# RWKV stage of a hybrid backbone on one core: TensorE in the emitted order, both halves of an inverse stage in one PSUM tile, and the parts of a unit at other places of its period

## The chip, the core and the metric

The kernel runs on one core of a Trainium2 chip. A core has a matrix engine (TensorE, called PE in the rows), VectorE (DVE), ScalarE (ACT), GpSimd (POOL) and SyncE (SP), which here issues DMAs; each works through its own list of instructions and waits at semaphores for the others. The metric is the device time of one execution in microseconds (us); the lower the better.

## The reference, cut to what matters

One trunk layer over 512 latent tokens with 256 context tokens ahead of them, model width 2048: a modulated norm, one input projection for three groups of recurrent heads (GLA, mLSTM, RWKV-7), one output projection, then a mixture of experts. The change lies in the RWKV heads, 12 of width 64 with one scan per direction:

```python
def _rwkv_scan(inp, s0):
    """RWKV-7: S = S diag(w) + (S (-kk)) (kk*a)^T + v k^T ; y = S r."""
    r, decay, k, v, kk, a = (jnp.moveaxis(t, 1, 0) for t in inp)
    def step(s, t):
        rt, wt, kt, vt, kkt, at = t
        sa = jnp.einsum('bhvk,bhk->bhv', s, -kkt)
        s = (s * wt[:, :, None, :] + sa[..., None] * (kkt * at)[:, :, None, :]
             + vt[..., None] * kt[:, :, None, :])
        return s, jnp.einsum('bhvk,bhk->bhv', s, rt)
    s_fin, ys = lax.scan(step, s0, (r, decay, k, v, kk, a))
    return jnp.moveaxis(ys, 0, 1), s_fin
```

Each output is then normalised per head, scaled, given a bonus term and gated:

```python
yr_l = (_head_norm(yl, g_norm, RWKV_GN_EPS, True) + bl) * jax.nn.sigmoid(gl)
```

## The kernel before

The scan is done in chunks of 64 tokens. A unit is one of three groups of four heads (two rows of 128 partitions, both directions) times one of six blocks of 128 tokens, so there are 18 units. A unit has three parts, each a Python generator that yields between pieces of its work.

`rw_s1` loads keys, values and decays (SyncE), forms decays by a product with a triangle (`pb`, the rows `g<-tri,rv_sgh`) and three exponentials on ScalarE (`ex`), multiplies them into `BK` and `AR` (VectorE and GpSimd), makes the key-query products `pA` in two rounds (rows `g<-AR,BK`), masks them on VectorE into `AMa` and `AMr` (L734), writes the 16x16 diagonal blocks of `AMa` to memory (`s_ad`, eight DMAs, L741) and reads them back in another layout (`Lay`, L742), and transposes `BK` (`pT`, L750).

`rw_s2` inverts a 64x64 triangle per chunk and head. First the 16x16 diagonal blocks: 15 steps of a product and a reduction on VectorE, `ptm<-Tm,Lay` (L776) and `Tm<-ptm` (L778), here called the T steps. The result goes through memory (`s_td`) by 16 DMAs into `ed`, two block-diagonal arrays `E` and `Dd`. Then four **inverse stages** on TensorE (L806), each a product over eight chunks: `Y` (from `Bo` and `Dd`, copied out of PSUM by ScalarE as `iY`, L810), `F1`, `F2` and `Ef` (each evacuated by VectorE with an addition, L812; the rows name the first two `iF`). A stage is emitted as two halves of four chunks, each half in a PSUM tile of its own under the tag "g", which has three buffers, with two yields in a half.

`rw_s3` carries the state through the unit's two chunks: `pX` (L833) gives `chX`, then `pSA` (L843) gives the two writes to `rv` (ScalarE L845, VectorE L846), then `pS` (L853) gives the new state `chS`. Every sixth unit ends with `rwkv_fin` for two rows of heads, four pieces in all with 256 columns each: a centering (L943), a square `fin_sq` on ScalarE, the sums `nb` (L152), a rsqrt chain on VectorE and GpSimd to `nb_x` (L159), its transposes (L167) and products.

`rwkv_all` runs periods: in period k it weaves `rw_s1` of unit k, `rw_s2` of unit k-1 and `rw_s3` of unit k-2 with `fill`, which is the rest of the input projection: matmuls `pl<-hil,wh` and the like (L329), six in a step, whose weights are split by ScalarE (`wh`, L306) and GpSimd or VectorE (`wl`, L307). `weave` gives each generator a number of steps and a share of the period and always advances the one that lags. What it emits is then ordered by a scheduler, which may move instructions against the emitted order by their priority; part of the projection's matmuls are emitted at high priority. The eight PSUM banks of this stage are: "g" three, "ch" two, "acc" one, "pl" two.

Of the kernel before, what the change touches and what calls it, by code (L numbers as in the profile page):

```python
# [19 lines left out]
P = 128  # L20
# [3 lines left out]
LC = 256  # L24
# [11 lines left out]
NS2 = 45  # L36
# [6 lines left out]
NKE = (12, 12, 12, 12)  # L43
# [5 lines left out]
W1, W2, W3 = (0, .9), (0, 1), (0, 1)  # L49


class Kern:
    def __init__(self, tc, I, out):
        self.tc, self.nc, self.I, self.out = tc, tc.nc, I, out
        self.dram = {}
        self.gt1 = None

# [20 lines left out]
    def load_consts(self, cp, ps):  # L78
# [42 lines left out]
        with self.tc.tile_pool(name="prow", bufs=1) as pr:  # L121
            done = 0
            rest = list(order)
            while done < tot:
# [12 lines left out]
                nc.tensor.transpose(p[:, :used], vr[:used], self.ident[:used, :used])  # L137
# [7 lines left out]
    def norm_bcast(self, pool, ps, tag, sq, nt, scale, eps, op, bufs=2):  # L145
# [5 lines left out]
        for t in range(nt):  # L151
            nc.tensor.matmul(pn[:, t], sq[:, t * P:(t + 1) * P], self.ind2, start=True, stop=True)  # L152
# [10 lines left out]
        for t0 in range(0, nt, 4):  # L163
            n = min(4, nt - t0)
            p = ps.tile([P, 512], F32, name=tag, bufs=bufs)
            for t in range(n):
                nc.tensor.transpose(p[:, t * P:(t + 1) * P], rx[:, t0 + t], self.ident)  # L167
# [3 lines left out]
    def phase_h(self, ps, early):  # L171
# [13 lines left out]
        with tc.tile_pool(name="wa", bufs=5) as wa, tc.tile_pool(name="xp", bufs=1) as xp:  # L185
            for t in range(6):
# [10 lines left out]
                for k0 in range(0, KT, 4):  # L197
                    p = ps.tile([P, 4, P], F32, name=("pl", "pc")[k0 // 4 % 2], bufs=self.pb)
                    for k in range(4):
                        nc.tensor.transpose(p[:, k], xt[:, (k0 + k) * P:(k0 + k + 1) * P], self.ident)  # L200
# [4 lines left out]
            for j in range(4):  # L205
                pa = ps.tile([P, 256], F32, name="px", bufs=2)
                for k0 in range(0, KT, 2):
# [3 lines left out]
                    for k in range(2):  # L211
                        for s in range(2):
                            for hf in range(2):
                                b = 32 * (2 * s + hf)
                                nc.tensor.matmul(pa[b:b + 32, :], self.sil[:, k0 + k, :], w[:, s, k, hf * 256:(hf + 1) * 256],
# [7 lines left out]
                for q in range(2):  # L223
                    nc.tensor.transpose(pt[:, q], ar[:, q * P:(q + 1) * P], self.ident)
# [36 lines left out]
    def ada2_sum(self, blk):  # L261
        nc = self.nc
        for q in range(4):
            p = self.ps.tile([P, 512], F32, name="px", bufs=2)
            nc.tensor.matmul(p[:1], self.ones[:, :1], self.acc2[:, q], start=True, stop=True)
# [44 lines left out]
    def w_tile(self, col, n, lat, ctx, fill=None):  # L310
# [4 lines left out]
        for q in range(4):  # L315
# [113 lines left out]
    def rw_k(self, pr):  # L429
# [25 lines left out]
        for d in range(2):  # L455
            yield
            a = sp.tile([P, T], F32, name="o_a")
            for (s0, n) in ((0, LC), (LC, S)):
                p = ps.tile([P, 512], F32, name="px", bufs=2)
                nc.tensor.matmul(p[:, :n], wz[:96, 1, d], self.wa1[:96, 2 + d, s0:s0 + n], start=True, stop=True)  # L460
# [11 lines left out]
            for t0 in (0, 4):  # L472
                n = min(4, 6 - t0)
                p = ps.tile([P, 4, P], F32, name="px", bufs=2)
                for t in range(n):
                    nc.tensor.matmul(p[:, t], self.wa1[:97, d, (t0 + t) * P:(t0 + t + 1) * P], wz[:, 0, d], start=True, stop=True)
# [20 lines left out]
    def to_tokens(self, x, o):  # L497
# [3 lines left out]
        for t0 in range(0, nt, 4):  # L501
            n = min(4, nt - t0)
            p = self.ps.tile([P, 4, P], F32, name=tag, bufs=bufs)
            for t in range(n):
                nc.tensor.transpose(p[:, t], x[:, (t0 + t) * P:(t0 + t + 1) * P], self.ident)
            nc.vector.tensor_copy(o[:, t0:t0 + n], p[:, :n])

    def rw_r(self, pr):
# [9 lines left out]
        nc.tensor.matmul(p, self.blk, m, start=True, stop=True)  # L518
# [145 lines left out]
    def rw_s1(self, st, u, q, g):  # L664
# [33 lines left out]
        for i in range(2):  # L698
            pb = ps.tile([P, 2, 2, 2, 64], F32, name="g", bufs=3)
            for d in range(2):  # L700
                for j, x in enumerate((sgh, sgl)):
                    nc.tensor.matmul(pb[:, d], x[:, i, d], self.tri, start=(j == 0), stop=(j == 1))
# [14 lines left out]
            yield  # L717
        n = 2 if g > 1 else 1
# [4 lines left out]
        for d in range(2):  # L723
            pA = [ps.tile([P, 4, n, 64], F32, name="g", bufs=3) for _ in range(2)]
            for c in range(4):
                for h in range(2):
                    hs = slice(64 * h, 64 * h + 64)
                    for a in range(2):
                        nc.tensor.matmul(pA[h][64 * a:64 * a + 64, c].rearrange("p a t -> p (a t)"), BK[hs, 4 * d + c, a],
                                         AR[hs, 4 * d + c, :n].rearrange("p a t -> p (a t)"), start=True, stop=True)  # L730
# [15 lines left out]
        pT = [ps.tile([P, 8, 64], F32, name="g", bufs=3) for _ in range(2)]  # L746
        for c in range(8):
            for h in range(2):
                hs = slice(64 * h, 64 * h + 64)
                nc.tensor.transpose(pT[h][:, c], BK[hs, c].rearrange("p a t -> p (a t)"), self.ident[hs, hs])  # L750
# [6 lines left out]
    def rw_s2(self, st, u):  # L757
# [8 lines left out]
        p = ps.tile([P, 8, 64], F32, name="g", bufs=3)  # L766
        for c in range(8):
            for h in range(2):
                hs, ks = slice(64 * h, 64 * h + 64), slice(64 - 64 * h, 128 - 64 * h)
                nc.tensor.matmul(p[hs, c], AMa[ks, h, c], RV[ks, h, c], start=True, stop=True)  # L770
# [13 lines left out]
        for j in range(2):  # L784
# [1328 lines left out]
```

## Time and profile before

| | |
|---|---|
| median of three runs | 3050.22 us (3045.81 to 3050.96) |
| the profiled execution | 3046.72 us, span 3045.0 us |
| mean granted clock of TensorE | 0.957 of full speed |
| TensorE busy | 2764.3 us, 91% of the span |
| VectorE busy | 1597.2 us, 52% |
| the RWKV stage | about 786 to 1560 us of the span |

The span is the profiled time between the first and the last instruction; the execution's own time is 1.7 us longer. [...]

### The profile page before, as it was taken

How to read it: one execution, taken by the hardware profiler on the slowest of the kernel's cores; microseconds unless marked ns; L12 is line 12 of the kernel's file. 1: busy time of each engine (PE TensorE's matmuls, PEld its weight loads, DVE VectorE, ACT ScalarE, POOL GpSimd, SP SyncE). 2: the span in 40 equal slices, each digit the busy share in tenths (PEclk: the TensorE clock that was granted, in tenths of full speed). 3: DMA queues.
4: the chain of work that ended last, by engine and by line, in shares of the span. 5: the costliest groups of instructions: out<-in, count | busy, mean ns of one | idle time of the engine just before them, and what ended most of it. 6: DMA issues, size and time to landing. Idle time of an engine off the chain costs nothing. (4 is left out here: it accounts for less than half of the span.)

```text
span 3045.0 us, 50599 instructions
## 1 busy us (share of the span) xinstructions
PE 2764.3 (91%) x19241; PEld 1811.1 (59%) x19241; DVE 1597.2 (52%) x3215; ACT 811.3 (27%) x1570; POOL 796.0 (26%) x765
## 2 busy tenths in 40 slices
PE   5999998989898998989968888879999999999997
PEld 3477777778676766767746666644444444444442
DVE  4376666686576555545547655643343433434335
ACT  4132332346432233222222322331021111211112
POOL 2332222221443343343344333431010110101101
PEclk8999999998999999999979999989999999999999
DMA  8857788887643343343266321459999999999997
GB/s 305 283 179 226 233 239 248 241 257 220 173 110 97 85 128 95 97 117 98 70 207 197 105 94 49 133 213 409 398 396 408 389 409 395 397 410 395 409 397 290
DMA packets 527741, 730.79 MB, mean 240 GB/s; under 512 B 121137, under 2 KB 343903, under 8 KB 526339
## 3 DMA queue, kind: packets, MB, share of 16 engines
q1 hardware_dynamic: 363696, 640.77, 58.8%
q10 hardware_dynamic: 161927, 81.17, 10.4%
q0 software_dynamic: 1872, 5.57, 0.6%
q8 instruction: 154, 2.52, 0.3%
q14 instruction: 92, 0.75, 0.1%
HBM read 672.50 MB, written 54.93 MB: 239 GB/s over the span
## 5 line engine op out<-in xcount | busy, mean ns | idle before, releaser
L1672 PE MATMUL pgu<-ring,xg 128*64 128x512 f32 x2048 | 480.6, 600 | 0.0
L307 POOL TENSOR_TENSOR wl<-wr,wh 128x512 fp32r<-128x512 f32 x191 | 263.2, 1379 | 668.8 <-ACT wh L306 600.7
L329 PE MATMUL pl<-hil,wh 128*128 128x512 f32 x928 | 404.4, 437 | 4.7 <-ACT hil L241 3.7
L329 PE MATMUL pl<-lol,wh 128*128 128x512 f32 x928 | 376.3, 405 | 0.2
L329 PE MATMUL pl<-hil,wl 128*128 128x512 f32 x928 | 372.4, 401 | 1.1 <-POOL wl L307 1.1
L306 ACT CAST wh<-wr 128x512 fp32r<-128x512 f32 x292 | 179.6, 619 | 528.0 <-PE pl L329 282.0
L1693 POOL TENSOR_TENSOR hl<-h,hh 128x512 fp32r<-128x512 f32 x64 | 83.9, 1311 | 809.7 <-ACT hh L1692 779.4
L1672 PEld LDWEIGHTS pgu<-ring,xg 128*64 128x64 f32 x2048 | 134.4, 136 | 237.3 <-issue 227.4
L1672 PE MATMUL py<-ring,hT 128*64 128x512 f32 x1024 | 230.4, 593 | 2.4 <-DMA ring<-in_moe_w_down_dram 2.4
L259 DVE SCALAR_TENSOR_TENSOR acc<-w,sil,acc 128x512 f32<-128x512 f32 x240 | 201.7, 870 | 58.5 <-DMA w<-in_w_ada_dram 57.6
L329 PEld LDWEIGHTS pl<-hil,wh 128*128 128x128 f32 x928 | 178.8, 193 | 60.7 <-issue 14.6
L329 PEld LDWEIGHTS pl<-hil,wl 128*128 128x128 f32 x928 | 178.8, 193 | 42.4 <-POOL wl L307 2.1
L329 PEld LDWEIGHTS pl<-lol,wh 128*128 128x128 f32 x928 | 179.6, 194 | 38.3 <-issue 6.4
L1672 PEld LDWEIGHTS py<-ring,hT 128*64 128x64 f32 x1024 | 76.7, 137 | 149.4 <-issue 141.9
L329 PE MATMUL pc<-hic,wl 128*128 128x256 f32 x496 | 146.9, 297 | 13.4 <-DVE wl L307 9.4
L329 PE MATMUL pc<-hic,wh 128*128 128x256 f32 x496 | 147.1, 298 | 4.7 <-ACT wh L306 2.6
L329 PE MATMUL pc<-loc,wh 128*128 128x256 f32 x496 | 146.1, 296 | 1.1 <-DVE loc L242 1.1
L1692 ACT CAST hh<-h 128x512 fp32r<-128x512 f32 x128 | 84.7, 663 | 193.7 <-POOL hl L1693 14.8
L776 DVE TENSOR_TENSOR ptm<-Tm,Lay 64x1 f32<-64x1 f32 (+2 forms) x270 | 105.5, 391 | 20.3 <-DMA Lay<-s_ad 10.1
L1410 POOL TENSOR_TENSOR wol<-wo,woh 128x512 fp32r<-128x512 f32 x56 | 74.9, 1341 | 155.8 <-PE acc L1413 91.3
L1763 DVE SCALAR_TENSOR_TENSOR yt<-py,Wsl,g 128x512 f32<-128x512 f32 x64 | 48.0, 750 | 127.4 <-PE py L1672 127.4
L1693 DVE TENSOR_TENSOR hl<-h,hh 128x512 fp32r<-128x512 f32 x64 | 53.2, 830 | 112.0 <-ACT hh L1692 109.5
(2216 smaller groups left out, 5011.6 us busy)
## 6 DMA issues: line engine op xcount, KB each, us to landing
ring<-in_moe_w_gate_dram SPq DMA_DIRECT2D x256, 512.0 KB
ring<-in_moe_w_up_dram SPq DMA_DIRECT2D x256, 512.0 KB
ring<-in_moe_w_down_dram SPq DMA_DIRECT2D x128, 1024.0 KB
wr<-in_w_in_dram ACTq DMA_DIRECT2D x288, 256.0 KB
w<-in_w_ada_dram SPq DMA_DIRECT2D x256, 256.0 KB
w<-in_w_ada_dram SPq DMA_DIRECT2D x64, 512.0 KB
wo<-in_w_out_dram SPq DMA_DIRECT2D x56, 256.0 KB
rv_xk<-d_xk SPq DMA_DIRECT2D x36, 256.0 KB
```

The costliest lines, as they stand in the source:

```text
L259: nc.vector.scalar_tensor_tensor(acc, w, self.sil[:, k, 0:1], acc, op0=OP.mult, op1=OP.add)
L306: nc.scalar.copy(wh[:, :, :n], wr[:, :, :n])
L307: (nc.vector if q in self.wdve else nc.gpsimd).tensor_tensor(wl[:, :, :n], wr[:, :, :n], wh[:, :, :n].bitcast(F32), op=OP.subtract)
L329: nc.tensor.matmul(o[:n], a[:, k, :n], r, start=(q == k == i == 0), stop=(q == k == 3 and i == 2))
L776: nc.vector.tensor_tensor(pt_[:, :t, :t], Tm[:, :t, :t], Lay[:, :t, t].rearrange("q (o s) -> q o s", o=1).to_broadcast([64, t, t]), op=OP. ...
L1410: nc.gpsimd.tensor_tensor(wl, w, wh.bitcast(F32), op=OP.subtract)
L1672: pin(nc.tensor.matmul(*a, **k))
L1692: nc.scalar.copy(hh, h)
L1693: (nc.gpsimd if k else nc.vector).tensor_tensor(hl, h, hh.bitcast(F32), op=OP.subtract)
L1763: nc.vector.scalar_tensor_tensor(yt, py, W, self.g2[:, col[0]:sum(col)], op0=OP.mult, op1=OP.mult)
```

## The change

First, every matmul and transpose goes through a helper (`mm`, `tr`), which during the RWKV stage pins it behind the TensorE instruction that was emitted before it; the high priority of the projection's matmuls goes. Second, `rw_s1` takes the first three quarters of a period and has more yields, between its rounds, and "g" has two buffers. Third, in `rw_s2` the product `XV` and the four inverse stages share one PSUM tile `g2` with one buffer: a stage's two halves lie in that one bank, are emitted one behind the other, and four yields follow. `Dd` is loaded ahead of `E`. Fourth, `rwkv_fin` leaves `rw_s3` and is a generator of its own in the next period, with its PSUM tiles under "ch". PSUM pools and step counts follow. The diff, cut; each remaining hunk only puts `self.mm` or `self.tr` in the place of the call:

```diff
-W1, W2, W3 = (0, .9), (0, 1), (0, 1)
+W1, W2, W3 = (0, .75), (0, 1), (0, 1)
-NS2 = 45
+NS2 = 50
-NKE = (12, 12, 12, 12)
+NKE = (12, 12, 10, 10, 8)
+NF = 40
+    def mm(self, *a, **k):
+        i = self.nc.tensor.matmul(*a, **k)
+        if self.pin:
+            self.tc.keep_in_program_order(i)
...
-                            first = k % self.wk == 0 and i == 0 or self.wk == 1
-                            with nullcontext() if first else self.tc.high_priority():
-                                nc.tensor.matmul(o[:n], a[:, k, :n], r, start=(q == k == i == 0), stop=(q == k == 3 and i == 2))
+                            self.mm(o[:n], a[:, k, :n], r, start=(q == k == i == 0), stop=(q == k == 3 and i == 2))
...
-            pb = ps.tile([P, 2, 2, 2, 64], F32, name="g", bufs=3)
+            pb = ps.tile([P, 2, 2, 2, 64], F32, name="g", bufs=2)
...
             nc.gpsimd.tensor_copy(W[:, cs], ex[:, 2, :, 63])
             yield
+            yield
...
                     nc.vector.tensor_tensor(o[:, h, 4 * d:4 * d + 4], pA[h][:, :, a], self.msk[:, a:a + 1].to_broadcast([P, 4, 64]), op=OP.mult)
+            yield
+            yield
...
-        p = ps.tile([P, 8, 64], F32, name="g", bufs=3)
+        p = ps.tile([P, 8, 64], F32, name="g2", bufs=1)
...
-        for j in range(2):
+        for j in (1, 0):
             src = self.s_td[u, j].rearrange("(c h i) (s t) -> i h s c t", h=2, i=4, s=16)
...
         for (o, lhs, rhs) in ((Y, Bo, Dd), (F1, Y, E), (F2, Y, F1), (Ef, Y, F2)):
+            p = ps.tile([P, 8, 64], F32, name="g2", bufs=1)
             for c0 in (0, 4):
                 sl = slice(c0, c0 + 4)
-                p = ps.tile([P, 4, 64], F32, name="g", bufs=3)
-                for c in range(4):
+                for c in range(c0, c0 + 4):
                     for h in range(2):
                         hs = slice(64 * h, 64 * h + 64)
-                        nc.tensor.matmul(p[hs, c], lhs[hs, c0 + c], rhs[hs, c0 + c], start=True, stop=True)
-                    if c % 2:
-                        yield
+                        self.mm(p[hs, c], lhs[hs, c], rhs[hs, c], start=True, stop=True)
                 if o is Y:
-                    nc.scalar.copy(Y[:, sl], p)
+                    nc.scalar.copy(Y[:, sl], p[:, sl])
                 else:
-                    nc.vector.tensor_tensor(o[:, sl], p, E[:, sl], op=OP.add)
+                    nc.vector.tensor_tensor(o[:, sl], p[:, sl], E[:, sl], op=OP.add)
+            for _ in range(4):
+                yield
...
-            if g == 5:
-                for i in range(2):
-                    yield from self.rwkv_fin(2 * q + i, self.rwy[:, i])
...
-        for k in range(n + 2):
+        def fins(q):
+            for i in range(2):
+                yield from self.rwkv_fin(2 * q + i, self.rwy[:, i])
+        for k in range(n + 3):
...
-            if k >= 2:
-                gs.append((self.rw_s3(st[k - 2], *units[k - 2]), 7 if units[k - 2][1] < 5 else 47, *W3))
+            if 2 <= k < n + 2:
+                gs.append((self.rw_s3(st[k - 2], *units[k - 2]), 7, *W3))
+            if k >= 3 and units[k - 3][1] == 5:
+                gs.append((fins(units[k - 3][0]), NF))
...
-                gs.append((self.rw_s1(st[k], k, *units[k]), 18, *W1))
+                gs.append((self.rw_s1(st[k], k, *units[k]), 24, *W1))
...
-            nb = yield from self.norm_bcast(mp, ps, "g", sq, 2, 1.0 / 64, 64e-5, OP.add, bufs=3)
+            nb = yield from self.norm_bcast(mp, ps, self.ft[0], sq, 2, 1.0 / 64, 64e-5, OP.add, bufs=self.ft[1])
...
+            self.pin = True
             drain([(self.rwkv_all(fill, NA * 16 // WK - RF), 1)])
+            self.pin = False
```

TensorE, stage F1 of an early unit, before. The names before the arrow are the tile written, behind it the tiles read; in brackets stand the semaphores that the row waits for, by the engine that raises them (DMAHW is a DMA), and L329 rows are the projection:

```order
L806 MATMUL g<-ed_6993,iY 64x64 [waits DMAHW5_49,Activation_49]
L806 MATMUL g<-ed_6993,iY 64x64 [waits DMAHW0_49]
L806 MATMUL g<-ed_6993,iY 64x64 x6
L806 MATMUL g<-ed_6993,iY 64x64 [waits Activation_49]
L806 MATMUL g<-ed_6993,iY 64x64 x7
L329 MATMUL pl<-hil,wh 128x512
L329 MATMUL pl<-lol,wh 128x512
L329 MATMUL pl<-hil,wl 128x512
L329 MATMUL pl<-hil,wh 128x512
L329 MATMUL pl<-lol,wh 128x512
L329 MATMUL pl<-hil,wl 128x512
L806 MATMUL g<-iF_7535,iY 64x64 [waits DVE_49]
```

The same stage in the changed kernel, where all matmuls have the helper's line, L61:

```order
L61 MATMUL g_8020<-ed_6993,iY 64x64 [waits DMAHW4_49,DMAHW6_49,DMAHW0_49,Activation_49]
L61 MATMUL g_8020<-ed_6993,iY 64x64 [waits DMAHW5_49,DMAHW7_49,DMAHW3_49,DMAHW1_49]
L61 MATMUL g_8020<-ed_6993,iY 64x64 x6
L61 MATMUL g_8020<-ed_6993,iY 64x64 [waits DVE_49]
L61 MATMUL g_8020<-ed_6993,iY 64x64 x7
L61 MATMUL pl<-hil,wh 128x512
L61 MATMUL pl<-lol,wh 128x512
L61 MATMUL pl<-hil,wl 128x512 [waits Pool_49]
L61 MATMUL pl<-hil,wh 128x512
L61 MATMUL pl<-lol,wh 128x512
L61 MATMUL pl<-hil,wl 128x512
L61 MATMUL g_8054<-iF_7985,iY 64x64 [waits DVE_49]
```

Before, the second half waits for ScalarE, which wrote the second half of its operand `iY`. Now it waits for VectorE, whose addition of the first half (`iF`) reads the tile `g_8020` that both halves write; six matmuls of the projection follow in both.

VectorE, the additions of F1 and F2 of a unit, before; `iF_8004` is F1, `iF_8005` is F2, `ptm` and `Tm` are the T steps of the next unit:

```order
L812 TENSOR_TENSOR iF_8004<-g,ed_6993 128x256 [waits DMAHW3_49,DMAHW4_49,DMAHW2_49,DMAHW5_49,DMAHW1_49,DMAHW6_49,DMAHW0_49,PE_49]
L812 TENSOR_TENSOR iF_8004<-g,ed_6993 128x256 [waits PE_49]
L550 SCALAR_TENSOR_TENSOR o_a<-pl,par,o_a 128x8x63 [waits DVE_49] x2
L812 TENSOR_TENSOR iF_8005<-g,ed_6993 128x256 [waits PE_49]
L776 TENSOR_TENSOR ptm<-Tm,Lay 64x1 [waits DMAHW7_49,Pool_49]
L812 TENSOR_TENSOR iF_8005<-g,ed_6993 128x256 [waits PE_49]
L778 TENSOR_REDUCE Tm<-ptm 64x1 [waits DVE_49]
```

A unit in the changed kernel, where `iF_8464` is F1:

```order
L823 TENSOR_TENSOR iF_8464<-g_8499,ed_6993 128x256 [waits DMAHW4_49,DMAHW5_49,DMAHW2_49,DMAHW6_49,DMAHW1_49,DMAHW7_49,DMAHW0_49,PE_49]
L290 TENSOR_TENSOR ar_t<-ar_t,ar_b 16x512 [waits DMAHW7_49,DMAHW0_49]
L789 TENSOR_TENSOR ptm<-Tm,Lay 64x1 [waits DMAHW1_49]
L291 SCALAR_TENSOR_TENSOR ar_t<-ar_t,ar_g 16x128 [waits DVE_49]
L823 TENSOR_TENSOR iF_8464<-g_8499,ed_6993 128x256 [waits PE_49]
L791 TENSOR_REDUCE Tm<-ptm 64x1 [waits DVE_49]
L873 TENSOR_TENSOR chW<-ch,chS 128x256 [waits PE_49]
L789 TENSOR_TENSOR ptm<-Tm,Lay 64x2x2 [waits DVE_49]
L791 TENSOR_REDUCE Tm<-ptm 64x2 [waits DVE_49]
L789 TENSOR_TENSOR ptm<-Tm,Lay 64x3x3 [waits DVE_49]
```

Before, the first T step, the one that waits for the DMA into `Lay`, stood between the two additions of F2. Now it stands between the two of F1, and further T steps come ahead of F2's additions.

TensorE, two of the last pieces of `rwkv_fin`, before:

```order
L152 MATMUL g<-k_ind_72,fin_sq 128x2 x2
L167 MATMUL g<-ident,nb_x 128x128 x2
L943 MATMUL g<-rv_y,k_blk 128x256
L152 MATMUL g<-k_ind_72,fin_sq 128x2 x2
L167 MATMUL g<-ident,nb_x 128x128 x2
```

And in the changed kernel:

```order
L61 MATMUL ch<-k_ind_72,fin_sq 128x2 x2
L61 MATMUL pl<-hil,wh 128x512
L61 MATMUL pl<-lol,wh 128x512
L61 MATMUL pl<-hil,wl 128x512
L61 MATMUL pl<-hil,wh 128x512
L61 MATMUL pl<-lol,wh 128x512
L61 MATMUL pl<-hil,wl 128x512
L66 MATMUL ch<-ident,nb_x 128x128 x2
```

Before, the transposes of `nb_x` came directly behind the sums `nb` from which they are worked out. Now six matmuls of the projection lie between them.

## Rows read from the trace of the kernel before

**Rows 1.** The page: the span, and busy time of each engine.

```profile
span 3045.0 us, 50599 instructions
...
PE 2764.3 (91%) x19241; PEld 1811.1 (59%) x19241; DVE 1597.2 (52%) x3215; ACT 811.3 (27%) x1570; POOL 796.0 (26%) x765
```

**Rows 2.** Windows: each stretch with its length, then busy us (instructions) by engine.

```profile
786.00:1560.00 774.00, 693.27 (x8434) 527.69 (x8432) 427.16 (x1124) 221.38 (x460) 304.27 (x340) 0.96 0.41 105
...
1980.00:3045.00 1065.00, 1018.06 (x4960) 464.31 (x4958) 425.24 (x743) 185.09 (x329) 108.71 (x92) 0.98 0.96 380
```

**Rows 3.** Groups of TensorE instructions in 786 to 1560 us, costliest first.

```profile
L329 PE MATMUL pl<-hil,wh 128*128 128x512 f32 x478 | 214.7, 449 | 0.0
...
L806 PE MATMUL g<-iF,iY 64*64 64x64 f32 x1152 | 45.4, 226 | 2.6 <-DVE iF L812 2.5
```

**Rows 4.** Waits of TensorE, 786 to 1560: total us, times, longest.

```profile
PE g L167 <- DVE nb_x L159: 14.7, 9, 2.9
PE ch L853 <- DVE rv L846: 14.0, 10, 3.7
PE g L729 <- POOL AR L713: 6.9, 5, 1.9
PE g L729 <- DVE AMr L734: 4.1, 3, 1.9
...
PE g L750 <- DVE AMr L734: 2.9, 1, 2.9
PE ch L853 <- ACT rv L845: 2.9, 2, 1.6
...
PE g L806 <- ACT iY L810: 0.2, 1, 0.2
```

**Rows 5.** Timeline of one unit's inverse stages and projections: start, length (us), engine.

```profile
1113.87 0.68 PE L806 MATMUL g<-ed,Bo 64*64 64x64 f32 x16
...
1114.60 0.37 ACT L810 COPY iY<-g 128x256 f32<-128x256 f32 x1 [0.24 <-PE g L806]
...
1115.78 0.40 PE L329 MATMUL pl<-lol,wh 128*128 128x512 f32 x1
...
1116.01 0.40 PE L329 MATMUL pl<-hil,wl 128*128 128x512 f32 x1
...
1116.34 1.15 PE L806 MATMUL g<-ed,iY 64*64 64x64 f32 x32
...
1117.07 0.92 DVE L812 TENSOR_TENSOR iF<-g,ed 128x256 f32<-128x256 f32 x2 [7.30 <-PE g L806]
```

**Rows 6.** Groups of the other engines in 786 to 1560 us.

```profile
L776 DVE TENSOR_TENSOR ptm<-Tm,Lay 64x1 f32<-64x1 f32 (+2 forms) x270 | 105.5, 391 | 20.3 <-DMA Lay<-s_ad 10.1 <-DMA rv<-d_vt 3.7
...
L778 DVE TENSOR_REDUCE Tm<-ptm 64x1 f32<-64x1 f32 (+2 forms) x270 | 62.0, 230 | 6.7
```

**Rows 7.** Timeline from the last key-query product to the first step of T.

```profile
1107.53 0.45 PE L729 MATMUL g<-AR,BK 64*64 64x128 f32 x8
...
1108.05 1.28 ACT L576 ACT_TABLE_LOAD   x1
...
1109.35 0.41 DVE L734 TENSOR_TENSOR AMr<-g,msk 128x256 f32<-128x256 f32 x1
...
1109.83 4.34 SPq L741 DMA_DIRECT2D s_ad<-AMa  x8
...
1116.06 0.48 SPq L742 DMA_DIRECT2D Lay<-s_ad  x1
...
1119.57 0.15 DVE L776 TENSOR_TENSOR ptm<-Tm,Lay 64x1 f32<-64x1 f32 x1 [1.59 <-DMA Lay<-s_ad]
```

**Rows 8.** Groups of ScalarE in 786 to 1560 us: the exponentials.

```profile
L707 ACT ACTIVATE ex<-g 128x256 f32<-128x256 f32 x36 | 13.8, 384 | 65.7 <-PE g L702 37.7 <-POOL W L716 13.6 <-DVE AR L715 8.0
```

**Rows 9.** Windows of 20 us with columns as in rows 2: two clock dips.

```profile
900.00:920.00 20.00, 19.62 (x169) 15.74 (x170) 14.67 (x32) 5.15 (x10) 8.66 (x9) 0.83 0.46 113
...
1180.00:1200.00 20.00, 16.90 (x187) 12.64 (x187) 4.14 (x12) 6.48 (x14) 5.66 (x5) 0.83 0.48 124
```

More of the change, by code (lines that the diff above doesn't have):

```diff
@@ L1 @@
 import math
-from contextlib import ExitStack, nullcontext
+from contextlib import ExitStack
 from functools import partial
@@ L151, in norm_bcast @@
         for t in range(nt):
-            nc.tensor.matmul(pn[:, t], sq[:, t * P:(t + 1) * P], self.ind2, start=True, stop=True)
+            self.mm(pn[:, t], sq[:, t * P:(t + 1) * P], self.ind2, start=True, stop=True)
         v = pool.tile([P, nt, 2], F32, name="nb_v")
@@ L264, in ada2_sum @@
             p = self.ps.tile([P, 512], F32, name="px", bufs=2)
-            nc.tensor.matmul(p[:1], self.ones[:, :1], self.acc2[:, q], start=True, stop=True)
+            self.mm(p[:1], self.ones[:, :1], self.acc2[:, q], start=True, stop=True)
             nc.scalar.copy(self.acc2[:1, q], p[:1])
@@ L517, in rw_r @@
         p = ps.tile([P, S], F32, name="px", bufs=2)
-        nc.tensor.matmul(p, self.blk, m, start=True, stop=True)
+        self.mm(p, self.blk, m, start=True, stop=True)
         nc.vector.tensor_tensor(m, self.vt[:, 0, LC:], p, op=OP.mult)
@@ L723, in rw_s1 @@
         for d in range(2):
-            pA = [ps.tile([P, 4, n, 64], F32, name="g", bufs=3) for _ in range(2)]
+            pA = [ps.tile([P, 4, n, 64], F32, name="g", bufs=2) for _ in range(2)]
             for c in range(4):
@@ L745, in rw_s1 @@
             nc.gpsimd.tensor_tensor(Bo[hs], AMa[hs, h], self.ndg[hs, None, :].to_broadcast([64, 8, 64]), op=OP.mult)
-        pT = [ps.tile([P, 8, 64], F32, name="g", bufs=3) for _ in range(2)]
+        pT = [ps.tile([P, 8, 64], F32, name="g", bufs=2) for _ in range(2)]
         for c in range(8):
@@ L769, in rw_s2 @@
                 hs, ks = slice(64 * h, 64 * h + 64), slice(64 - 64 * h, 128 - 64 * h)
-                nc.tensor.matmul(p[hs, c], AMa[ks, h, c], RV[ks, h, c], start=True, stop=True)
+                self.mm(p[hs, c], AMa[ks, h, c], RV[ks, h, c], start=True, stop=True)
             if c % 2:
@@ L832, in rw_s3 @@
                     for hs in H:
-                        nc.tensor.matmul(pX[hs, e], AR[hs, 2 * e + c, 0], St[hs, e], start=True, stop=True)
+                        self.mm(pX[hs, e], AR[hs, 2 * e + c, 0], St[hs, e], start=True, stop=True)
                 if g > 1:
@@ L842, in rw_s3 @@
                 for hs in H:
-                    nc.tensor.matmul(pSA[hs, e], Ef[hs, 2 * e + c], X[hs, e], start=True, stop=True)
+                    self.mm(pSA[hs, e], Ef[hs, 2 * e + c], X[hs, e], start=True, stop=True)
             rv = RV.rearrange("p h (e c) k -> p h e c k", c=2)
@@ L864, in rw_s3 @@
                     for h in range(2):
-                        nc.tensor.matmul(pYo[H[h], 2 * e + c], RV[:, h, 2 * e + c], AMr[:, h, 2 * e + c], start=False, stop=(c == 1 and e == 3))
+                        self.mm(pYo[H[h], 2 * e + c], RV[:, h, 2 * e + c], AMr[:, h, 2 * e + c], start=False, stop=(c == 1 and e == 3))
             yield
@@ L941, in center @@
         nc = self.nc
-        p = self.ps.tile([P, y.shape[1]], F32, name="g", bufs=3)
-        nc.tensor.matmul(p, m, y, start=True, stop=True)
+        p = self.ps.tile([P, y.shape[1]], F32, name=self.ft[0], bufs=self.ft[1])
+        self.mm(p, m, y, start=True, stop=True)
         nc.vector.scalar_tensor_tensor(y, p, -scale, y, op0=OP.mult, op1=OP.add)
@@ L1034, in ml_gates @@
         for j in range(6):
-            nc.tensor.matmul(p[:, j], selp[:, j], dm[:, 1], start=True, stop=True)
+            self.mm(p[:, j], selp[:, j], dm[:, 1], start=True, stop=True)
         nc.vector.tensor_copy(self.mdec, p)
@@ L1252, in gla_pair @@
                     for i in range(2):
-                        nc.tensor.matmul(p, la[:, i, t], lev[:, c0:c0 + 384], start=(i == 0), stop=(i == 1))
+                        self.mm(p, la[:, i, t], lev[:, c0:c0 + 384], start=(i == 0), stop=(i == 1))
                     if j == 0:
@@ L1412, in out_cols @@
                     for t in range(4):
-                        nc.tensor.matmul(po[t], a[:, i, t * P:(t + 1) * P], b, start=(i == j == 0), stop=(i == n - 1 and j == 2))
+                        self.mm(po[t], a[:, i, t * P:(t + 1) * P], b, start=(i == j == 0), stop=(i == n - 1 and j == 2))
                 yield
@@ L1455, in out_last @@
                     for j, (a, b) in enumerate(((yh, wh), (yl, wh), (yh, wl))):
-                        nc.tensor.matmul(p, a[:, i, t * P:(t + 1) * P], b[:, i, cs], start=(i == j == 0), stop=(i == n - 1 and j == 2))
+                        self.mm(p, a[:, i, t * P:(t + 1) * P], b[:, i, cs], start=(i == j == 0), stop=(i == n - 1 and j == 2))
                 nc.vector.tensor_tensor(self.x1[:, t, cs], self.x1[:, t, cs], p, op=OP.add)
@@ L1480, in route_setup @@
         p = self.ps.tile([P, 36], F32, name="lt", bufs=1)
-        nc.tensor.matmul(p, self.ones, sr, start=True, stop=True)
+        self.mm(p, self.ones, sr, start=True, stop=True)
         nc.vector.tensor_tensor(self.cb, self.cb, p, op=OP.add)
@@ L1577, in route_slots @@
         for t in range(4):
-            nc.tensor.matmul(pc, ltb[:, 1], Ab[:, t], start=(t == 0), stop=(t == 3))
+            self.mm(pc, ltb[:, 1], Ab[:, t], start=(t == 0), stop=(t == 3))
         self.over = rp.tile([P, 32, 7], F32, name="over")
```

74 lines of the change are left out of this document (41 added, 33 removed).

## The prediction

> **What bounds the kernel now.** I began with the page: TensorE is busy for 91% of the span [rows 1], so time is lost or won where it idles, switches or runs at half clock. The windows then split the span. In the RWKV stage, 774 us long, TensorE is busy for 693.27 us with a granted clock of 0.96, so about 81 us are idle and about 31 us (4% of 774) are lost to the lower clock level [rows 2]. The last stage is busy for 1018 of 1065 us and the change doesn't touch it [rows 2]. TensorE's order ahead of the RWKV stage is the same in both programs and behind it nearly so; I put every term into the 774 us.
>
> Inside the stage the projection is the bulk: one of its three groups is 214.7 us [rows 3]. It depends on nothing in a unit, so it can fill any gap that the order leaves for it. That makes the list of waits the view to read next. Its 23 rows, from 14.7 us down to 0.2, sum to 69 us: 14.7 for `nb_x` in the final norm, 16.9 for `rv` in the state chain (14.0 and 2.9), 6.9 for `AR`, 7.0 for `AMr` under the products and the transposes (4.1 and 2.9), the rest in small rows [rows 4]. The inverse stages, which the change rebuilds, hardly wait: 2.6 us idle ahead of 1152 matmuls of the later stages [rows 3]. The reader should see that the change can win at most some 69 us of waits, part of 31 us of clock, and the switches below.
>
> **The change part by part.**
>
> *The emitted order.* Counted in the two orders of TensorE, changes between the projection's wide matmuls and narrow ones fall from 592 to 497 in the stage. Two projection rows start 0.23 us apart, but the narrow F1 starts 0.33 us after the last of them [rows 5], so a switch costs 0.10: 95 x 0.10 = 9.5 us won. The amount of matmul work is the same.
>
> *Waits that go.* In the final norm the new order puts at least six and mostly twelve projection matmuls (1.4 to 2.8 us by the 0.23 of [rows 5]) with other work between `nb` and the transposes; the longest wait there was 2.9 [rows 4], so I take 13 of 14.7. For `rv` the distance grows by some 0.4 to 0.8 us at each of 12 waits: 8 of 16.9. The added yields put about 1 us between the rounds of `pA` and ahead of `pT`: 5 of the 7.0 for `AMr`. The distance from `pb` to `pA` in the second round stays as it was: 2 of the 6.9 for `AR`. Of the remaining 24 I take half, 12. Together 40 us won; the bounds are 25 (only the norm, half of `rv` and of the masks) and 69 (all).
>
> *The shared tile.* This is the cost that I weigh most. In the changed order the second half of Y waits for ScalarE, and of F1, F2 and Ef for VectorE, with the evacuation of the stage's own first half as what they wait for, because both lie in one tile. TensorE's order is fixed, so nothing behind it, the six projection matmuls included, can pass. The price comes from one row each. The 16 records of Y start at 1113.87 and last 0.68; a single one lasts 0.226 (the mean of the same shape in [rows 3]), so the last is issued at about 1114.32, and ScalarE's copy ends at 1114.60 + 0.37 = 1114.97 [rows 5]: 0.65 us, in which only 0.03 of issue would have passed anyway. So 0.62 for Y. VectorE's addition takes 0.05 more (0.42, a half of the pair's 0.92 less the small gap) [rows 5]: 0.67 for each of three. A unit pays 0.62 + 3 x 0.67 = 2.63 us, 18 units 47.4, rounded 48. Before, each half had its own bank and the price was nothing. The bounds: 48 if VectorE and ScalarE are always free, more in the next term; less only as far as an earlier wait would have been in the same place, which the 2.6 us of [rows 3] caps.
>
> [...]
>
> *VectorE's queue.* F2's first half needs F1's second addition, and now its second half needs F2's first addition. T steps of the next unit stand between those. An operation of a T step takes on average (105.5 + 62.0) / 540 = 0.31 us [rows 6]. Between F1's second addition and F2's first one the new order has 4 to 13 of them in 14 of the 18 units; TensorE gets there after six projection matmuls and a half stage, about 2.0 us. Where n x 0.31 is above 2.0 the rest is waited for: 14 us over all units. The early steps are shorter than the mean (0.15 us for the first [rows 7]), which could leave 4. Before, the same additions had a stage's whole spacing to be late in, since no half waited for the other.
>
> *T behind Lay.* In most units the first T step stands ahead of F1's second addition and itself waits for `Lay`. In [rows 7] it starts 12.0 us after the last group of `pA` began (1107.53 to 1119.57), or 11.6 after its end, since eight DMAs are issued for 4.34 us and `Lay` behind them. In the new order there are 12 projection matmuls (2.8 us), 48 narrow ones (96 records at 0.036, the 1.15 / 32 of F1 in [rows 5]: 3.5) and eight switches (0.8) from that end to F1's first half, plus Y's half wait, two additions and F1's own: 9.7 us to F1's second addition. If `Lay` comes as in [rows 7], TensorE waits 1.9 us in about 13 units, 25 us; if TensorE's other stalls (or a less busy SyncE) close the distance, nothing. I take 4: every stall above delays F1 against `Lay`. With the 14 of the queue that is 18; the bounds of both together are 4 and 39.
>
> *Two buffers for "g".* The second tile of `pA` now needs the bank of the second `pb`, which three exponentials must have read: 3 x 0.384 = 1.15 us [rows 8]. The distance stays at about 2.1 us, so it is hidden unless ScalarE loads a table in between, 1.28 us [rows 7]; then some 0.5 is waited for. I take 8 us (18 x 0.45); the bounds are 0 and 9.
>
> *Clock.* Dips such as 0.83 over 900 to 920 and 1180 to 1200 us [rows 9] cost 3.4 us each. In the second TensorE had been busy for only 16.90 of 20 us. Evenly spread idle time replaces clustered waits, but total idle time does not fall much. I take 10 of the 31 us as won; the bounds are 0 and 20.
>
> *No cost.* Loading `Dd` first only advances what Y needs and delays E, whose stage is later. That the final norm runs a period later is hidden by the next group's units, except for the last group, whose norm stood at the end of the stage before as well. The six projection steps moved by `NKE` stay within the stage. The `ch` tag gets the norm's tiles, with two buffers; if one comes late it is the state chain that waits, which the bound of 25 on the won waits includes.
>
> **The sum.** -9.5 - 40 + 48 + 18 + 8 - 10 = +14.5 us. The profiled execution took 3046.72 us, so 3061.2; the median shown is 3.5 us above it, so 3064.7 on that scale, rounded 3065.
>
> **The rivals.** *Faster:* the half waits stand in for the old ones. They give every evacuation 2.6 us a unit more lead, so all 69 us of waits go (29 more) and T has its `Lay` in time with only the 4 us of queue left (14 less): 3065 - 43 = 3022; half of that gives 3043. For it: the waits of [rows 4] are short, mean 1.4 us. Against it: they have different places, few behind an inverse stage. It decides from the point at which `Lay` lands within 9.7 us of the last `pA`. *Same:* the queue term is 4 and the buffers cost 0, which takes 22 off, or about 3045 to 3055 with the errors of the wait terms. *Much slower:* `Lay` comes as in [rows 7] throughout and VectorE, held by T, delays `rv` and the masks too: 21 more for the queue, 15 fewer waits won: 3101. *The change does nothing:* if TensorE mostly went in emitted order before and the projection hides the half waits, the time stays; the fixed order speaks against it, since six projection matmuls stand behind, not between, the halves.
>
> **How the numbers follow.** 0.2% of this time, about 6 us, is what a measurement here can tell from no change. The forecast, slower by 6 to 30 us, has 0.42; much slower 0.13; the same 0.15 (with "does nothing"); faster 0.30. The time is the forecast's, 3065; its own range is 3056 to 3081. For 8 in 10 the range reaches from 3022, where the faster rival has its full terms, to 3098.
>
> **What the profile after would show.** Right: some 72 waits of the inverse stages' second halves, 18 of them on ScalarE and 54 on VectorE, near 0.65 us each and about 48 us together; `nb_x` down to 1 or 2 us; further waits of these stages of 1 to 3 us where a T step or `Lay` comes ahead. Wrong: waits of the inverse stages well under 30 us in total, which would mean that the halves do not wait or that the price is less than an evacuation; a stage clock at 0.99 or higher, a third of my gain too small; or 60 us of the old waits gone.

## The result and the profile after

The changed kernel is slower: 3095.78 us in the median of four runs (3085.98 to 3099.28) against 3048.01 of the kernel before, a ratio of 1.0152 with a 95% interval of 1.0127 to 1.0178, some 46 us. The direction of the prediction held, and the time lies inside its wide range (3022 to 3098), but outside the forecast's own (3056 to 3081): the loss is three times the 14.5 us of its sum. The profiled execution is the fastest of the four, 39 us longer in its span than the one of [rows 1]. The page of the changed kernel:

```profile
span 3084.2 us, 50665 instructions
...
PE 2765.7 (90%) x19241; PEld 1807.5 (59%) x19241; DVE 1593.8 (52%) x3215; ACT 818.8 (27%) x1576; POOL 791.6 (26%) x765
```

TensorE is busy as long as before; it idles longer. To set the stage of the two beside each other without the tail behind it, each window below ends behind the last `nb_x` of the final norm. The columns are those of [rows 2]. Before:

```profile
786.00:1550.00 764.00, 693.27 (x8434) 527.69 (x8432) 426.68 (x1123) 221.38 (x460) 302.67 (x336) 0.96 0.41 103
```

After:

```profile
786.00:1589.00 803.00, 693.96 (x8429) 523.86 (x8430) 418.76 (x1119) 229.25 (x465) 293.38 (x332) 0.94 0.38 96
```

The stretch is 39 us longer, busy time is the same (693.27 and 693.96), so the whole difference is idle time (the length less TensorE's busy time): 70.7 us before, 109.0 after. The granted clock went from 0.96 to 0.94, not up. The waits of TensorE in the stage after (total, times, longest), which answer to [rows 4]:

```profile
PE g L61 <- DVE iF L823: 25.8, 29, 3.0
PE g L61 <- ACT iY L821: 21.8, 19, 3.2
PE g L66 <- DVE AMr L745: 14.5, 10, 3.6
PE g L61 <- DVE Ef L823: 14.0, 17, 1.8
PE g L61 <- ACT rv_sgh L689: 7.5, 1, 7.5
PE g L61 <- DMA ed<-s_td: 6.8, 3, 3.3
PE ch L61 <- DVE rv L859: 3.8, 3, 2.9
PE g L61 <- DVE AMr L745: 3.2, 4, 1.8
PE g L61 <- DVE ptm L789: 2.8, 5, 0.7
PE g L61 <- ACT ex L719: 2.6, 3, 1.8
...
PE g L61 <- DVE Tm L791: 2.0, 3, 1.0
PE ch L66 <- DVE nb_x L171: 1.8, 5, 0.8
```

The view's 17 rows sum to 112 us, against 69. The one long wait for `rv_sgh` began before the window did:

```profile
789.41 0.58 PE L61 MATMUL g<-tri,rv_sgh 128*128 128x256 f32 x1 [7.46 <-ACT rv_sgh L689]
```

It started at 781.95, so 4.1 us of it lie ahead of 786, and the waits inside the stage are 108 us. The waits that rank highest in [rows 4] are nearly gone: `nb_x` 1.8 for 14.7, `rv` 3.8 for 16.9, `AR` none for 6.9. In their place stand the inverse stages: 25.8 + 21.8 + 14.0 + 6.8 + 2.8 + 2.0 = 73.2 us on `iF`, `iY`, `Ef`, `ed` and the T steps, which waited for 8.5 us before, and the masks: `AMr` under the transposes is 14.5 for 2.9.

One unit's F2 and Ef in the timeline after show how (start, length, engine; in brackets the idle time before it):

```profile
1099.06 0.68 PE L61 MATMUL g<-iF,iY 64*64 64x64 f32 x16
...
1099.64 0.69 DVE L319 TENSOR_TENSOR wl<-wr,wh 128x512 fp32r<-128x512 f32 x1 [0.29 <-ACT wh L318]
...
1100.24 0.42 DVE L823 TENSOR_TENSOR iF<-g,ed 128x256 f32<-128x256 f32 x1
...
1100.72 0.68 PE L61 MATMUL g<-iF,iY 64*64 64x64 f32 x16 [0.98 <-DVE iF L823]
...
1102.92 0.68 PE L61 MATMUL g<-iF,iY 64*64 64x64 f32 x16
...
1103.67 0.41 DVE L823 TENSOR_TENSOR Ef<-g,ed 128x256 f32<-128x256 f32 x1
...
1104.13 0.68 PE L61 MATMUL g<-iF,iY 64*64 64x64 f32 x16 [0.54 <-DVE Ef L823]
```

The first half of F2 starts at 1099.06. Its addition comes only at 1100.24, behind other work of VectorE (here `wl`, a weight of the projection), and the second half, which needs nothing but the tile, starts at 1100.72. For Ef nothing is late: 1102.92, addition at 1103.67, second half at 1104.13. Taken over all 72 stages, the distance from the start of a first half's last matmul to the start of its second half is 0.69 us at least, mostly 0.75, and 82 us in total; the prediction's 0.65 was the wait of the undisturbed ones. Of the idle time in front of the inverse stages' matmuls, 66 us lie ahead of second halves and 6 ahead of first ones.

### The profile page after: what moved, and what is told of

Its sections match the earlier page's. It is cut to its first block, busy times and chain, and to the rows that moved or that the text cites. A ratio compares the mean times of both kernels' runs of the same rounds, so it can differ in the third digit from the quotient of the medians.

```text
span 3084.2 us, 50665 instructions
## 1 busy us (share of the span) xinstructions
PE 2765.7 (90%) x19241; PEld 1807.5 (59%) x19241; DVE 1593.8 (52%) x3215; ACT 818.8 (27%) x1576; POOL 791.6 (26%) x765
## 5 line engine op out<-in xcount | busy, mean ns | idle before, releaser
L61 PE MATMUL pl<-hil,wh 128*128 128x512 f32 x928 | 408.9, 441 | 4.4 <-ACT hil L253 3.7
L61 PE MATMUL pl<-lol,wh 128*128 128x512 f32 x928 | 379.3, 409 | 0.1
L61 PE MATMUL pl<-hil,wl 128*128 128x512 f32 x928 | 374.8, 404 | 0.4 <-POOL wl L319 0.4
L61 PEld LDWEIGHTS pl<-hil,wh 128*128 128x128 f32 x928 | 180.2, 195 | 60.8 <-issue 14.8
L61 PEld LDWEIGHTS pl<-hil,wl 128*128 128x128 f32 x928 | 180.7, 195 | 42.1 <-issue 1.2
L61 PEld LDWEIGHTS pl<-lol,wh 128*128 128x128 f32 x928 | 181.6, 196 | 37.3 <-issue 6.0
L61 PE MATMUL pc<-hic,wl 128*128 128x256 f32 x496 | 146.4, 296 | 13.0 <-POOL wl L319 7.2
L61 PE MATMUL pc<-hic,wh 128*128 128x256 f32 x496 | 146.8, 297 | 4.5 <-ACT wh L318 2.6
L61 PE MATMUL pc<-loc,wh 128*128 128x256 f32 x496 | 145.8, 295 | 1.1 <-DVE loc L254 1.1
L1709 ACT CAST hh<-h 128x512 fp32r<-128x512 f32 x128 | 84.8, 663 | 193.5 <-POOL hl L1710 14.5
L319 DVE TENSOR_TENSOR wl<-wr,wh 128x512 fp32r<-128x512 f32 x101 | 74.0, 735 | 83.6 <-ACT wh L318 77.9
```

The source lines that it names most:

```text
L61: i = self.nc.tensor.matmul(*a, **k)
L319: (nc.vector if q in self.wdve else nc.gpsimd).tensor_tensor(wl[:, :, :n], wr[:, :, :n], wh[:, :, :n].bitcast(F32), op=OP.subtract)
L1709: nc.scalar.copy(hh, h)
```

## The experiments

Ratios are to the kernel before, run on the same chip; times in us against it are the ratio's distance from 1 times 3048. Theory A is the prediction's: the half waits cost, and with them what is queued. Rival B is that the fixed order of TensorE costs wherever something is late.

**One evacuation per stage.** In the changed kernel, each stage is copied or added once, behind both halves:

```diff
-                if o is Y:
-                    nc.scalar.copy(Y[:, sl], p[:, sl])
-                else:
-                    nc.vector.tensor_tensor(o[:, sl], p[:, sl], E[:, sl], op=OP.add)
+            if o is Y:
+                nc.scalar.copy(Y, p)
+            else:
+                nc.vector.tensor_tensor(o, p, E, op=OP.add)
```

> The changed kernel, with each inverse stage evacuated once, after both halves, instead of once per half. Theory A (the half waits and what they drag along: 72 x about 0.7 us, part of the addition's queue, and the clock that idle time costs): the gap between halves falls from 0.75 us to 0.05, the stage's one evacuation lies behind six projection matmuls, and the time falls by 50 to 70 us against the changed kernel, to about 3030 to 3045, below the kernel before. Rival B (a fixed order of TensorE is what costs; the wait only shows at the halves and will show at the next stage, which needs the same data): less than 15 us saved, about 3085.

Measured: ratio 0.9957 (0.9941 to 0.9974), 59 us below the change (1.0152 to 0.9957), as theory A expected. The half distances fall to 0.05 us, 3.8 in total. Its stage, to just behind the last `nb_x`, and its largest waits:

```profile
786.00:1551.00 765.00, 681.55 (x8442) 521.27 (x8442) 417.06 (x1068) 223.74 (x448) 300.91 (x336) 0.94 0.40 103
```

```profile
PE g L61 <- DVE iF L823: 20.2, 10, 4.2
PE g L61 <- ACT iY L821: 14.0, 6, 3.9
PE g L61 <- DMA ed<-s_td: 13.6, 5, 5.1
...
PE g L66 <- DVE AMr L745: 3.9, 5, 1.6
```

What is left of the inverse stages' waits, 47.8 us in the first three rows, lies between stages, on data: there the six projection matmuls don't always reach. Ahead of first halves TensorE idled for 6 us in the change and for 47 here. So rival B has a part in it: more than half of the wait came back at the next stage, and the profiled stage is 38 us shorter (765 for 803), not the 78 by which the half distances fell. In time theory A holds for the change as it stands. The run also has fewer evacuations, each twice as large; what that alone does in a fixed order no run shows.

**Each half in its own bank**, under "g" with three buffers again, as are the other tiles of "g" and `XV`; the diff, cut:

```diff
...
-            p = ps.tile([P, 8, 64], F32, name="g2", bufs=1)
             for c0 in (0, 4):
+                p = ps.tile([P, 4, 64], F32, name="g", bufs=3)
...
```

> The changed kernel, with each half of an inverse stage in a PSUM tile of its own under the tag g, which has three buffers again; order, evacuations and all else as in the change. Theory A: the halves no longer wait for each other, 45 to 65 us saved against the changed kernel, about 3030 to 3050; the third buffer may add up to 8. Rival B: the order is as fixed as in the change, so about 3085 or more.

Measured: 1.0045 (1.0028 to 1.0062), 33 us below the change, about half of what the single evacuation gave. The halves of F1, F2 and Ef no longer wait (0.05 us each), but Y's second half does:

```profile
PE g L61 <- ACT iY L821: 50.7, 17, 7.2
...
PE g L66 <- DVE AMr L745: 3.5, 2, 3.3
```

Y's tiles are now in the same ring of three buffers as the two `pT` tiles of the next unit. One unit in the timeline:

```profile
1084.20 0.34 PE L66 MATMUL g<-ident,BK 64*128 64x64 f32 x4
...
1084.98 0.63 PE L61 MATMUL g<-ed,Bo 64*64 64x64 f32 x16
...
1088.54 0.62 ACT L689 CAST rv_sgh<-rv_sg 128x512 fp32r<-128x512 f32 x1 [8.14 <-DMA rv_sg<-d_sg]
...
1091.52 0.37 ACT L821 COPY iY<-g 128x256 f32<-128x256 f32 x1 [1.57 <-POOL wl L319]
1091.95 1.12 PE L61 MATMUL g<-ed,Bo 64*64 64x64 f32 x16 [6.33 <-ACT iY L821]
1093.00 0.69 PE L66 MATMUL g<-ident,BK 64*128 64x64 f32 x8
```

Half of the transposes into the `pT` tiles stand ahead of Y and half behind it, so these two tiles are still being filled and Y's halves are left with one buffer. The second half waits for ScalarE's copy of the first one, as in the change: in all 17 waits it starts some 0.05 us behind the end of that copy. Here ScalarE comes late to it, behind a cast (`rv_sgh`) that itself waits for a DMA. The distances between Y's halves alone, measured as above, sum to 54.8 us, for 25.4 in the change. So for Y this run did not part the halves; the wait moved from the shared tile to the ring. Neither expectation was met: theory A had 45 to 65 us, rival B none.

**Without the pin**, all else as in the change:

```diff
-            self.pin = True
+            self.pin = False
```

> The changed kernel without the pinning of TensorE to the emitted order; the shared tile stays. Theory A: the scheduler can put projection matmuls between the two halves, which hides the wait while the bank stays shared: 30 to 60 us saved, about 3035 to 3065, and gaps between halves of about 1.7 us filled by six projection matmuls. Rival B expects the same size, so this run alone does not tell them apart; rival C (the shared tile costs whatever stands between) expects less than 15.

Measured: 0.9910 (0.9875 to 0.9945), 74 us below the change and faster than the kernel before. That is more than the 30 to 60 us of theory A and far from the less than 15 of rival C. Stage and waits:

```profile
786.00:1518.00 732.00, 690.09 (x8407) 509.27 (x8406) 419.89 (x1117) 228.86 (x465) 297.87 (x330) 0.97 0.41 105
```

```profile
PE g L61 <- ACT iY L821: 16.6, 10, 3.1
...
PE g L61 <- DVE iF L823: 3.1, 8, 1.0
```

The same pair of halves (Ef of a unit) in its timeline:

```profile
1067.33 0.68 PE L61 MATMUL g<-iF,iY 64*64 64x64 f32 x16
...
1067.94 0.50 PE L61 MATMUL pl<-hil,wl 128*128 128x512 f32 x1
...
1068.06 0.42 DVE L823 TENSOR_TENSOR Ef<-g,ed 128x256 f32<-128x256 f32 x1
1068.28 0.40 PE L61 MATMUL pl<-hil,wh 128*128 128x512 f32 x1
...
1068.52 0.40 PE L61 MATMUL pl<-lol,wh 128*128 128x512 f32 x1
...
1068.76 0.40 PE L61 MATMUL pl<-hil,wl 128*128 128x512 f32 x1
...
1069.08 0.68 PE L61 MATMUL g<-iF,iY 64*64 64x64 f32 x16
```

Four projection matmuls stand between the halves. From start to start the halves are 1.75 us apart, for 1.21 in the change (1102.92 to 1104.13), and it costs nothing, since TensorE works through it. The stage is 71 us shorter than in the change; 67 of these are idle time (41.9 us for 109.0), only 4 are busy time.

**The pin alone**, on the kernel before: every matmul and transpose of the stage kept in the emitted order by the helpers of the change, each half with its own bank as before. The diff, cut to the place that sets it:

```diff
...
+            self.pin = True
             drain([(self.rwkv_all(fill, NA * 16 // WK - RF), 1)])
+            self.pin = False
```

> The kernel before, with every matmul and transpose of the RWKV stage pinned to the emitted order, and nothing else of the change. Theory A: each half has its bank, so the pin alone costs little: 3040 to 3065, with some waits where a later stage stands directly behind an earlier one. Rival B: most of the change's loss is here already, 3080 to 3100.

Measured: 1.0183 (1.0166 to 1.0200), 56 us slower. Theory A's expectation for this run failed; B's came out, and somewhat beyond it: without any shared tile the fixed order alone loses more than the whole change. Its waits and its stage, up to the last `nb_x`:

```profile
PE g L65 <- DVE AMr L745: 20.4, 11, 4.6
PE ch L60 <- DVE rv L857: 13.9, 9, 2.9
PE g L60 <- DMA ed<-s_td: 12.9, 3, 4.4
```

```profile
786.00:1614.00 828.00, 725.79 (x8433) 538.93 (x8433) 436.36 (x1121) 224.30 (x461) 293.62 (x334) 0.92 0.37 94
```

100 us of waits instead of 69, at places that the shared tile has nothing to do with, and TensorE busy for 725.79 us at a granted clock of 0.92 (693.27 at 0.96 before). Of the 64 us by which the stage is longer, half is idle time and half busy time. How much of the busy half is clock the granted clock alone does not tell: the version with own banks has 0.92 too and is busy for less than before (its window ends 12 us behind the last `nb_x`).

```profile
786.00:1578.00 792.00, 687.86 (x8434) 523.88 (x8435) 417.76 (x1121) 227.13 (x465) 298.01 (x337) 0.92 0.39 100
```

**One evacuation and no pin**, the changed kernel with the edits of the first and the third run together:

```diff
-            self.pin = True
+            self.pin = False
...
-                    nc.scalar.copy(Y[:, sl], p[:, sl])
+                nc.scalar.copy(Y, p)
...
```

> The changed kernel with one evacuation per inverse stage and without the pin. Theory A (two costs: the half waits, which a free order hides, and the fixed order, which lets every other wait stand open): the half waits are gone already by one of the two, so against the version that only lost the pin (0.991 of before) the gain is small, 0 to 15 us, ratio to before 0.985 to 0.992; against the pinned version with one evacuation (0.9957) 10 to 30 us better. Rival B (the pin costs only through the halves): as the pinned version with one evacuation, 0.994 to 0.998.

Measured: 0.9907 (0.9881 to 0.9932), the same as without the pin alone. When the order is free, the split evacuation in a shared tile costs nothing that the intervals (some 13 us) would show. Nor does the shared tile itself: the version below with the second and fourth part, own banks and no pin is at 0.9922.

**The projection free, the rest pinned.** In the changed kernel, one call goes back to the unpinned form:

```diff
-                            self.mm(o[:n], a[:, k, :n], r, start=(q == k == i == 0), stop=(q == k == 3 and i == 2))
+                            nc.tensor.matmul(o[:n], a[:, k, :n], r, start=(q == k == i == 0), stop=(q == k == 3 and i == 2))
```

> The changed kernel with everything pinned but the projection's matmuls, which the scheduler may move; units' matmuls stay in the emitted order, the shared tile stays. Theory A (the fixed order costs because the projection, which depends on nothing here, can't go into the gaps): it gives back most of the pin's price, 50 to 76 us against the changed kernel, 3020 to 3045, with projection matmuls between the halves. Rival B (the order among the units' own matmuls is what costs): less than 30 us back, 3065 or more.

Measured: 0.9975 (0.9954 to 0.9996), 54 us below the change, with the units' own matmuls still in the emitted order and the shared tile in place. Waits:

```profile
PE g L61 <- ACT iY L821: 14.0, 8, 3.5
PE g L61 <- DVE iF L823: 10.6, 11, 2.5
PE g L61 <- DVE Ef L823: 4.0, 6, 1.0
```

28.6 us on `iY`, `iF` and `Ef` for 61.6. So about three quarters of the pin's price of 74 us are that the projection can't pass. The remaining 20, known to some 12 us either way, belong to the units' own order.

**The other parts, one by one on the kernel before, without pin.** The final norm as its own generator, with the step counts that go with it; the diff, cut:

```diff
-            if g == 5:
-                for i in range(2):
-                    yield from self.rwkv_fin(2 * q + i, self.rwy[:, i])
...
+            if k >= 3 and units[k - 3][1] == 5:
+                gs.append((fins(units[k - 3][0]), NF))
```

> The kernel before with only the fourth part: the final norm as a generator of its own in the next period, its PSUM tiles still under g. The waits for nb_x were 14.7 us and those for rv stand partly in the same places. If this part makes most of what the unpinned change wins (32 us): ratio 0.990 to 0.994. If the win is spread or comes from elsewhere: 0.995 to 1.000.

Measured: 0.9968 (0.9954 to 0.9983), 10 us won. `rw_s1` in three quarters with its yields; the diff, cut:

```diff
-W1, W2, W3 = (0, .9), (0, 1), (0, 1)
+W1, W2, W3 = (0, .75), (0, 1), (0, 1)
...
-                gs.append((self.rw_s1(st[k], k, *units[k]), 18, *W1))
+                gs.append((self.rw_s1(st[k], k, *units[k]), 24, *W1))
```

> The kernel before with only the second part's timing: rw_s1 in three quarters of a period, 24 steps, and its added yields; g keeps three buffers. If earlier masks, and with them an earlier Lay and earlier T steps, make most of the unpinned win: ratio 0.990 to 0.994. Otherwise 0.995 to 1.003.

Measured: 0.9915 (0.9885 to 0.9945), 26 us won. Both edits together:

> The kernel before with the second and the fourth part of the change and neither the pin nor the shared tile: rw_s1 in three quarters with its yields, the final norm in the next period, three buffers of g, each half of a stage with its own bank. The two alone gave ratios 0.9915 and 0.9968. If they add: 0.986 to 0.990, the fastest so far. If they win the same waits: 0.990 to 0.993.

Measured: 0.9922 (0.9891 to 0.9952): they don't add. Only the share, with no added yield:

```diff
-W1, W2, W3 = (0, .9), (0, 1), (0, 1)
+W1, W2, W3 = (0, .75), (0, 1), (0, 1)
```

> The kernel before with only the share of rw_s1 set to three quarters of a period, with no yield added and 18 steps as before. If the earlier end of rw_s1 (earlier masks, Lay and T steps) makes the win of the second part: ratio 0.990 to 0.994. If the added yields between its rounds make it: 0.996 to 1.002.

Measured: 0.9912 (0.9880 to 0.9944), 27 us won by one number. That is the whole of the second part, and as much as the whole change wins without its pin (0.9910). Its stage, and its largest waits:

```profile
786.00:1520.00 734.00, 664.61 (x8411) 507.60 (x8409) 426.55 (x1121) 219.88 (x458) 294.55 (x333) 0.97 0.41 106
```

```profile
PE g L806 <- DVE iF L812: 18.6, 23, 2.3
PE g L167 <- DVE nb_x L159: 12.9, 10, 2.6
```

The waits sum to 68 us as before (69); it is busy time that is shorter, 664.61 for 693.27. Which work got cheaper these rows don't tell. The clock is little of it: counted in the clock records of the two traces, TensorE was busy at its lower level (a granted share of 0.5 in the records of the trace before) for 40 us of this stage and for 53 before. And without the projection's high priority:

```diff
-                            with nullcontext() if first else self.tc.high_priority():
+                            with nullcontext():
```

> The kernel before without the high priority of the projection's matmuls, which the change also removes. If that priority is what keeps six projection matmuls together at the wrong places, the time falls: ratio 0.990 to 0.996. If it does what it is there for, more switches between wide and narrow matmuls at 0.1 us each, 0 to 15 us longer: 1.000 to 1.005.

Measured: 1.0002 (0.9981 to 1.0023). It does nothing here.

## Why the prediction was right in sign and wrong in size

**The shared tile, VectorE's queue and T behind Lay** (48 + 18 = 66 us). Right in mechanism and size: the inverse stages waited 73.2 us after and 8.5 before, 65 more, nearly all of it at second halves, 18 of them on ScalarE and 54 on VectorE as said. For one Ef the trace shows the second half start 0.05 us behind the end of the addition that reads the other half (1103.67 + 0.41 = 1104.08, then 1104.13); whether two halves in one tile could do without this wait no run shows. Of the 82 us of half distances 28 lie above 0.75 a stage: some 16 on VectorE, where 14 were booked for its queue, and some 12 on ScalarE's copies of Y, where none were. The term names its own condition, that the order is fixed and nothing can pass, but books the price to the tile. That condition is the pin: unpinned, the same tile costs nothing that the runs show (0.9910 with it, 0.9922 with own banks, the intervals some 10 us either way).

**Waits that go** (40 us) and **two buffers** (8 us), net 32 won. Measured: inside the stage all waits but those of the inverse stages went from 60.6 to 35.0 us, 25.6 won. The norm gave 13 as said, `rv` 13 for the 8 booked, `AR` 6.9 for the 2 booked. What failed is "5 of the 7.0 for `AMr`": the masks' waits did not shrink, they grew to 17.7, 14.5 of it ahead of the transposes of `pT`. Why is open. With two buffers a `pT` tile can be held up by the masks that read `pA`, but the runs don't follow the buffers: pinned with three buffers this row is 3.5 in one run and 20.4 in another, pinned with two and one evacuation 3.9. The place at which I put the buffers' 8 us, the second tile of `pA`, shows 2.6 on `ex`.

**Clock** (10 us won). Failed. The granted clock fell from 0.96 to 0.94 and busy time did not fall. I argued that evenly spread idle time replaces clustered waits; there is simply more idle time, 109.0 us for 70.7. That clustered idle time is what lowers the clock no run shows. Counted in the clock records, TensorE was busy at the lower level for 78 us of the stage, for 53 before. Two projection matmuls start 0.233 us apart at full clock and 0.427 at the lower one (medians in the trace before), so as an estimate some 11 us more were lost where 10 were to be won.

**Switches** (9.5 us won). Failed as counted. Neighbours of which one is a projection matmul and the other is not number 427 in the trace before and 461 after, so by the term's own price there was nothing to win. Nor does the number by itself order the times: the unpinned version has 610, some 15 us more than the change by the 0.10 of the prediction, and is 74 us faster, since it idles for 67 us less.

On the profiles the sum was 14.5 for 39. Of the 25 us missing some 5 are waits (34 booked, 39 measured) and 20 are clock and switches: 19.5 were booked as won, and busy time is 693.96 us for 693.27. The 46 us between the medians are 7 more, which no trace shows: the profiled execution is the fastest of its four, 10 us below their median. The "much slower" rival gave nearly the measured time, but by luck and not by its mechanism: `rv` did not come back, and the T steps held TensorE for only 4.8 us directly.

The step that failed is the one headed "The emitted order": it was entered as a gain, of switches and with them of clock, and its own price, on waits other than the half waits, was put at nothing. I put the gains of the new places and the price of the shared tile into one list as if the fixed order came free. The runs separate them: the earlier `rw_s1` alone wins 27 us, the pin alone loses 56, and the pin under the change's own order loses 74, of which some 54 is that the projection is pinned too. The split evacuation is the other half of that loss: one evacuation per stage gives back 59 with the pin in place. Either edit alone turns the loss into a gain, and the two together win no more than the free order alone. "The change does nothing", the rival that asked whether TensorE went in emitted order before, should have led me to ask what the scheduler's moves were worth: in the trace of before, about half of the later stages have six projection matmuls between their halves, 1.74 us by the same measure as above, and the others none, 0.05.

Open stay two things: why the earlier `rw_s1` shortens TensorE's busy time at equal waits, and what a different clock alone would be worth, since no run changed it alone.

## What to carry to other kernels

Work that depends on nothing is worth as much as the freedom to place it: before fixing an engine's order, ask for every wait in it what could pass, and leave the independent work unpinned. Splitting an evacuation in halves won nothing in any run here; in one tile, in a fixed order, each split mostly put 0.75 us between the halves for 0.05 with one evacuation, and with the order free it cost nothing that the runs show (0.9910 split, 0.9907 with one evacuation). A wait that is taken away at one place can come back at the next: here more than half of it did. When a change has several parts, price each as if it were alone: here one number of one part won as much as the whole change without its pin.

## What the runs showed of the hardware that was not expected

The pinned version of the kernel before is busy for 33 us longer with the same matmuls, at a granted clock of 0.92 for 0.96, while it idles for 32 us more. Counted in the clock records, TensorE was busy at the lower level for 104 us of the stage, for 53 before; by the two distances of projection matmuls above (0.233 and 0.427 us), some 23 of the 33 us are clock, as an estimate. Idle time alone does not set the clock: in the changed kernel it went down by less, to 0.94, with more idle time (109 us for 102). Nor does the granted clock of a stage set its busy time: at the same 0.92, the version with own banks was busy for 687.86 us and the pinned one for 725.79.
